# Four weight tiles with each token block at the start of a streaming encoder's first projection, in place of two

## The chip, the cores and the metric

The kernel runs on one core of a Trainium2 chip. A core has five engines, each with an instruction queue of its own that it works through in order: TensorE (PE) multiplies 128x128 tiles of weights with columns of activations into PSUM banks, VectorE (DVE) and ScalarE (ACT) work on tiles of 128 partitions, GpSimd (POOL) does small work and starts transfers, SyncE (SP) starts most transfers. The engines wait for each other through semaphores. The metric is the device time of one execution in microseconds (us), the median of several runs.

## The reference

One layer of a hybrid streaming encoder runs over 1024 prompt frames, 16 meta tokens ahead of them and 32 frames of a running stream, 1072 tokens together. All of it is in float32. The part that the change touches is the beginning:

```python
def rmsnorm(x, g):
    xf = x.astype(jnp.float32)
    r = lax.rsqrt(jnp.mean(xf * xf, axis=-1, keepdims=True) + EPS)
    return (xf * r).astype(x.dtype) * g

def project(h, w_in):
    z = h @ w_in
    a_in, q, k, v = jnp.split(z, [2 * D_CONV, 2 * D_CONV + D_ATTN, 2 * D_CONV + D_ATTN + D_KV], axis=-1)
    glu = a_in[..., :D_CONV] * jax.nn.sigmoid(a_in[..., D_CONV:])
...
def conv_module(glu_ext, dw_w, dw_b, ln_g, ln_b):
    y = depthwise_causal_conv(glu_ext, dw_w, dw_b)
    return jax.nn.silu(layernorm(y, ln_g, ln_b))
```

Each token is normalized by the root of its mean square over 1024 channels and projected to 1792 columns: 1024 for a gated unit (512 gates, 512 values), 512 for queries, 128 for keys and 128 for values. The gated unit goes through a causal convolution over 31 tokens for each channel; queries, keys and values go through windowed attention. An output projection, a gated feed-forward part and a last norm follow; the change leaves these alone.

## The kernel before

Activations are held with channels on the partitions and tokens along the columns. The 1792 columns of the first projection are 14 weight tiles of 128 columns; each has eight pieces `k` of 128 channels. Tiles 0 to 7 are gates and values of the gated unit in turn (an even tile a gate, the odd one behind it its value), 8 and 9 keys and values, 10 to 13 queries. The tokens are three blocks, `TB`: block 0 has 336 columns, block 1 has 384, block 2 has 352.

To come near float32, every operand is split into a high part (rounded to TensorE's fast format) and a low part (what the rounding left). A product is three matmuls: high by high, high by low, low by high (L252 to L254). ACT makes a high part, DVE the low part. For a weight tile of the first loads that is `split` (L246, L247); for x, multiplied by the norm's gain, it is L338 and L339. For later weight tiles, `wsplit` has ACT write the high part and the negated source (L237, L241), and a transfer started by GpSimd adds the source to it (L242).

The norm's factor isn't applied to x ahead of the projection but to its result. So the matmuls start without it, but no result can leave PSUM until it is there. For each block ACT squares the eight pieces of x (L359) and DVE adds seven of the squares into a row of sums (L362). Then `rms_first`, driven by `RM`, does three things in PE's order: three matmuls with ones sum over the partitions (L268, called the sums here), with the root taken by DVE and GpSimd behind them (L271 to L279); ACT scales the identity by the factor (L283, the diagonals); three matmuls with ones spread the factor over all partitions (L289, the spread), and ACT copies it to `rb` (L349). `RM` gives, for each block, the slots at which these happen; a slot is one `k` of one weight tile and block.

`START` is the order of the first groups: tiles 0 and 1 with block 0 side by side, then tile 0 with blocks 1 and 2, then tile 1 with blocks 1 and 2. Behind that, tiles go in `ORDER`, each with blocks 0, 1, 2, and each fetched two ahead. `NPRE` tiles stand ahead of the attention, the last two run inside of it. A finished group waits in `pend`; `flush` takes it out of PSUM once the block's factor is there (`in_evac`): a gate is multiplied by the factor (L572), goes through a sigmoid on ACT (L574) and is multiplied by the factor again (L631), then the value is multiplied by it (L577).

The convolution is 31 multiply-adds on DVE for each channel tile and stretch of tokens, the taps (L397, L400), queued in `tapq` and let out by budgets: `TGS` in the start, `TGW` behind it, with 1000.0 for all that are there. Some taps of channel tile 0 go through ACT and a GpSimd transfer (`chain_taps`, one after each group of the blocks in `CHG`).

PE's order is written out by hand in the start, and from `region` behind it on PE's and ACT's. Elsewhere a scheduler orders each engine's queue by a simulated timeline; DVE's order is always the scheduler's. SP's loads go out in the order of L330 to L332: two half weight tiles, two pieces of x, two half tiles, six more pieces of x, then blocks 1 and 2.

Of the kernel before, what the change touches and what calls it, by code (L numbers as in the profile page):

```python
# [166 lines left out]
def body(nc, tc, cp, wp, xp, dp, io):  # L167
# [150 lines left out]
    for i in range(WRM):  # L318
        nc.tensor.matmul(warm[:, 0:P], ones, ones, start=True, stop=True)

    nc.scalar.dma_start(prm, d.prm)
    for b, (t0, n) in enumerate(TB):
        if b == 0:
            pre = [[wp.tile([P, 1024], F32 if t == "raw" else F32R, tag=t, name=t) for t in ("raw", "whi", "wlo")]
                   for c in range(2)]
        for k in range(0, KD, 2):
            if b == 0 and k % 4 == 0:
                for c in range(2):
                    raw, hi, lo = (z[:, k * P:k * P + 512] for z in pre[c])
                    nc.sync.dma_start(raw, d.win[c, :, k:k + 4].rearrange("p a b -> p (a b)"))  # L330
                    split(hi, lo, raw)
            nc.sync.dma_start(X[b][:, k:k + 2, :], d.xT[:, k:k + 2, t0:t0 + n])  # L332
        if b == 0:
            pre = [z[1:] for z in pre]
        if b == 0:
            nc.scalar.dma_start(ident, d.cst[:, 0, :])
        for k in range(KD):
            hid[b, k] = nc.scalar.activation(HI[b][:, k, :], X[b][:, k, :], AF.Copy, scale=pcol("g1", k)).ins  # L338
            cast[b, k] = nc.vector.scalar_tensor_tensor(out=LO[b][:, k, :], in0=X[b][:, k, :], scalar=pcol("g1", k),  # L339
                                                        in1=HI[b][:, k, :].bitcast(F32), op0=ALU.mult,  # L340
                                                        op1=ALU.subtract).ins
    rms1 = []

    def rms_first(b, parts):
# [5 lines left out]
        ready.append(b)  # L350
        yield

    for b, (t0, n) in enumerate(TB):
        parts = [acc[:, p, t0:t0 + n] for p in (1, 0)[:NSUM]]
        for k in range(KD):
            sq = pd.tile([P, 384], F32, tag="sqs", name="sq", bufs=6)[:, :n]
            to = parts[k % NSUM] if k < NSUM else sq
            with tc.issue_after(hid[SQB[b]]):
                nc.scalar.activation(to, X[b][:, k, :], AF.Square)  # L359
            if k >= NSUM:  # L360
                with tc.issue_after(cast[SQD[b]]):
                    nc.vector.tensor_tensor(out=parts[k % NSUM], in0=parts[k % NSUM], in1=sq, op=ALU.add)  # L362
        rms1.append(rms_first(b, parts))

    close(cD)
    cA, pc_ = pool("ca", "left")
    CA = new(pc_, "ca", 4, T)
    cD, pd = pool("d2", "left")
    qpt = new(pd, "qp", 2, 2 * SEQ)
    qp = qpt.rearrange("p j (c a i) -> p j c a i", a=2, i=CHUNK)  # L370
    qs = new(pd, "qs", 4, NS)
    qm = new(pd, "qm", 4, NMETA)
    nc.gpsimd.memset(qm, 0.0)
    kT = new(pd, "kT", KW)
    vT = glu[:, 3, 0:KW]
    vsx = new(pd, "vsx", NS)
    bt = [new(pd, f"bt{i}", 4, SCW) for i in range(3)]
    bsm = new(pd, "bsm", 2, SSW)
    bme = new(pd, "bme", 17)
    mv = new(pd, "mv", 4, NMETA)  # L380
    va = new(pd, "va", NCH, P)
    vb = new(pd, "vb", NCH - 1, P)
    sm = new(pd, "sm", 36)
    vsa = new(pd, "vsa", P)
    vsb = new(pd, "vsb", P)
    ptb = [glu[:, 0, i * 512:i * 512 + 512].rearrange("p (a b) -> p a b", a=2) for i in range(2)]
    pb = [glu[:, 1, i * SCW:i * SCW + SCW] for i in range(2)] + [new(pd, f"pb{i}", SCW) for i in range(NPB - 2)]
    ksx = new(pd, "ksx", SSW)
# [170 lines left out]

# [3 lines left out]
    def in_evac(c, b, ps):  # L563
        t0, n = TB[b]
        r = rb[b]
        if c < 8:
            p = c // 2
            for lo_, hi_, o in pieces(b, CW - 1, SOFF):
                g = glu[:, p, o:o + hi_ - lo_]
                rs = r[:, lo_:hi_]  # L570
                if c % 2 == 0:
                    gate.append(nc.vector.tensor_tensor(out=g, in0=ps[:, lo_:hi_], in1=rs, op=ALU.mult))  # L572
                    if c in ORDER[:NPRE] or c == 0:
                        nc.scalar.activation(g, g, AF.Sigmoid)  # L574
                        defer.append((g, rs))
                else:
                    gate.append(nc.vector.tensor_tensor(out=g, in0=ps[:, lo_:hi_], in1=g, op=ALU.mult))  # L577
# [103 lines left out]
    region = tc.manual_schedule(engines={mybir.EngineType.PE})  # L681
    region.__enter__()
    for step in START:
        if step == START[-3]:
            spots += ["pt1", "pt0", "o"]
        for ps in zip(*(in_mm(b, pre[c]) for c, b in step)):
            pass
        pend += [(c, b, p) for (c, b), p in zip(step, ps)]
        flush()
        taps(TGS[step[0][1]], gate[-1].ins if gate else None)  # L690
    region.__exit__(None, None, None)
# [1133 lines left out]
```

## Time and profile before

| what | value |
|---|---|
| median of three runs | 1055.53 us (1055.09 to 1056.13) |
| the profiled execution | 1056.16 us |
| its span, first to last instruction | 1054.4 us |
| PE busy | 1031.6 us, 98% of the span |
| DVE busy | 864.4 us, 82% |
| ACT busy | 508.7 us, 48% |
| GpSimd busy | 161.2 us, 15% |
| mean granted clock of TensorE | 0.997 |

A row of a timeline gives start, length, engine, line, operation, result and operands by their names in the program, shape and count; in brackets stands the idle time ahead of it and what ended it. Matmuls overlap, so what one costs is the distance between two starts, not its length. A matmul on plain float32 operands shows as two rows of count.

### The profile page before, as it was taken

The numbers are of one execution on the slowest core, as the hardware profiler recorded it, in microseconds if no ns is written. First come the engines' busy times: TensorE is split into PE (matmuls) and PEld (weight loads), VectorE is DVE, ScalarE is ACT, GpSimd is POOL, SyncE is SP. The second block draws the span as 40 slices with busy tenths as digits, with TensorE's granted clock in tenths as the row PEclk, the third lists the DMA queues.
The fourth block names the chain that finished last, engine by engine and source line by source line (L and its number), as shares of the span: only waits on it lengthen the run. The fifth ranks groups of instructions, "written<-read, shape, count | busy, mean of one in ns | idle before, by whom it ended". The sixth has DMA issues, their size and how long they took to land.

```text
span 1054.4 us, 19959 instructions
## 1 busy us (share of the span) xinstructions
PE 1031.6 (98%) x7741; PEld 1005.2 (95%) x7741; DVE 864.4 (82%) x1643; ACT 508.7 (48%) x1068; POOL 161.2 (15%) x203
## 2 busy tenths in 40 slices
PE   9999999889999999999999999999999999999996
PEld 9999997658999999999999999999999999999996
DVE  7999998899978978888887888888778876985636
ACT  8653336897676744433333443343336722532333
POOL 1133120002425220001000000100110041000042
PEclk9999999999999999999999999999999999999998
DMA  7388673124963123243233233232326794732204
GB/s 267 89 172 165 148 153 71 41 47 65 168 156 107 65 79 102 71 139 97 71 114 120 63 102 116 88 102 88 116 81 209 241 188 122 245 125 81 61 4 162
DMA packets 69559, 123.88 MB, mean 117 GB/s; under 512 B 10448, under 2 KB 43464, under 8 KB 69464
## 3 DMA queue, kind: packets, MB, share of 16 engines
q1 hardware_dynamic: 56376, 96.78, 28.4%
q0 software_dynamic: 12128, 24.95, 13.9%
q8 instruction: 61, 1.00, 0.4%
q10 hardware_dynamic: 960, 0.87, 0.3%
q14 instruction: 34, 0.28, 0.1%
HBM read 78.90 MB, written 27.51 MB: 101 GB/s over the span
## 4 chain that ended last, share of the span: by engine, by line
PE 86%; DVE 6%; ACT 5%; DMA 2%; issue 1%; DVEq 0%; SPq 0%; ACTq 0%
PE mm L1281 53%; PE mm L252 10%; PE mm L254 10%; PE mm L253 10%; DVE acc L400 1%; ACT pb L763 1%; ACT glu L827 1%; PE R L289 1%; DMA raw<-wdn 1%; DVE bl L1218 1%; DMA raw<-woc 1%; ACT hi L338 1%; PE R L268 1%; DMA xs<-xT 0%; DMA prm<-prm 0%
## 5 line engine op out<-in xcount | busy, mean ns | idle before, releaser
L1281 PE MATMUL mm<-bh,sl 128*128 128x264 f32 (+1 forms) x912 | 214.0, 284 | 0.0
L1281 PEld LDWEIGHTS mm<-bh,sl 128*128 128x128 f32 x912 | 157.2, 188 | 0.0
L400 DVE SCALAR_TENSOR_TENSOR acc<-glu,prm,acc 128x324 f32<-128x324 f32 (+4 forms) x190 | 155.1, 844 | 1.1
L1281 PE MATMUL mm<-bl,sl 128*128 128x264 f32 (+1 forms) x424 | 121.0, 285 | 0.4 <-DVE bl L1218 0.4
L1281 PE MATMUL mm<-th,rawr 128*128 128x264 f32 x640 | 120.0, 284 | 0.0
L1281 PE MATMUL mm<-bh,wlo 128*128 128x264 f32 (+1 forms) x440 | 117.6, 284 | 0.0
L1281 PE MATMUL mm<-bh,whi 128*128 128x264 f32 (+1 forms) x440 | 112.6, 284 | 1.0 <-DVE x L1423 1.0
L1423 DVE TENSOR_TENSOR x<-x,mm 128x264 f32<-128x264 f32 (+7 forms) x238 | 76.1, 346 | 43.6 <-PE mm L1281 43.3
L252 PE MATMUL mm<-hi,whi 128*128 128x352 f32 (+3 forms) x312 | 103.9, 333 | 0.0
L254 PE MATMUL mm<-hi,wlo 128*128 128x352 f32 (+3 forms) x312 | 101.1, 324 | 0.0
L253 PE MATMUL mm<-lo,whi 128*128 128x352 f32 (+3 forms) x312 | 101.1, 324 | 0.0
L1281 PEld LDWEIGHTS mm<-th,rawr 128*128 128x128 f32 x640 | 100.4, 188 | 0.0
L1281 PE MATMUL mm<-th,sl 128*128 128x264 f32 x352 | 92.7, 284 | 0.0
L1281 PE MATMUL mm<-tl,rawr 128*128 128x264 f32 x320 | 90.8, 284 | 0.0
L1281 PEld LDWEIGHTS mm<-bh,wlo 128*128 128x128 f32 x440 | 80.6, 188 | 0.0
L1281 PEld LDWEIGHTS mm<-bl,sl 128*128 128x128 f32 x424 | 79.9, 188 | 0.6 <-DVE bl L1218 0.6
L1281 PEld LDWEIGHTS mm<-bh,whi 128*128 128x128 f32 x440 | 79.0, 188 | 1.2 <-ACT sl L1217 1.2
L1281 PE MATMUL mm<-bl,whi 128*128 128x264 f32 (+1 forms) x272 | 77.5, 285 | 0.0
L1217 ACT CAST sl<-x 128x512 fp32r<-128x512 f32 (+1 forms) x41 | 29.7, 727 | 73.6 <-DMA x<-wup 37.5
L1281 PEld LDWEIGHTS mm<-th,sl 128*128 128x128 f32 x352 | 63.8, 188 | 0.0
L1281 PEld LDWEIGHTS mm<-tl,rawr 128*128 128x128 f32 x320 | 60.3, 188 | 0.0
L252 PEld LDWEIGHTS mm<-hi,whi 128*128 128x128 f32 x312 | 58.7, 188 | 1.0 <-issue 0.6
(362 smaller groups left out, 2918.3 us busy)
## 6 DMA issues: line engine op xcount, KB each, us to landing
x<-wup SPq DMA_DIRECT2D x20, 512.0 KB, 4.4
x<-wup SPq DMA_DIRECT2D x40, 256.0 KB, 2.8
yq<-x SPq DMA_DIRECT2D x32, 264.0 KB, 2.8
wlo<-raw POOLq DMA_DIRECT2D x16, 512.0 KB, 4.6
ca<-ca POOLq DMA_DIRECT2D x18, 383.0 KB, 5.2
raw<-win SPq DMA_DIRECT2D x12, 512.0 KB, 4.4
raw<-wdn SPq DMA_DIRECT2D x12, 512.0 KB, 3.5
rb<-yq SPq DMA_DIRECT2D x10, 528.0 KB, 4.6
```

Of the source, the lines that this page charges most:

```text
L252: nc.tensor.matmul(ps, whi(k), xhi(k), start=first and i == 0, stop=False)
L253: nc.tensor.matmul(ps, whi(k), xlo(k), start=False, stop=False)
L254: nc.tensor.matmul(ps, wlo(k), xhi(k), start=False, stop=last and i == n - 1)
L268: nc.tensor.matmul(ss[:, i:i + 1], z[:, at:at + P], ones[:, 0:1], start=j == 0, stop=j == len(parts) - 1)
L289: nc.tensor.matmul(R[:, at:at + P], left[i], diag[i], start=True, stop=True)
L338: hid[b, k] = nc.scalar.activation(HI[b][:, k, :], X[b][:, k, :], AF.Copy, scale=pcol("g1", k)).ins
L400: nc.vector.scalar_tensor_tensor(out=a, in0=e[:, a0 + k:a1 + k], scalar=pcol("cw", p * CW + k), in1=a, op0=ALU.mult, op1=ALU.add)
L763: nc.scalar.activation(qs_[i], qs_[i], AF.Exp, bias=m[0][:, i:i + 1], scale=-1.0, accum_out=m[1][:, i:i + 1])
L827: nc.scalar.copy(ptb[kv], pts[kv])
L1217: nc.scalar.copy(hi, raw)
L1281: nc.tensor.matmul(ps, w[:, j, :], x[:, j, :], start=first and j + i == 0, stop=j == 3 and i == 2, skip_group_check=True)
L1423: summed[0] = nc.vector.tensor_tensor(out=z, in0=z, in1=ps[:, lo_:hi_], op=ALU.add).ins
```

## The change

Tiles 2 and 3 join tiles 0 and 1 in the start, and its order is now by block: four tiles with block 0, then four with block 1, then four with block 2. `ORDER` loses 2 and 3 and `NPRE` goes from 10 to 8, so the tiles ahead of the attention are the same. Tile 4 comes next, then 5, 8, 9, 10 and so on; before, 8 and 9 stood ahead of 4.

All first loads, splits and squares are written out, and ACT's order is by hand from the beginning. The parameters come in two transfers: the eight columns of the first gain on ACT's queue, the rest on SP's, where the identity's load goes too. Tiles 2 and 3 are split by ACT and DVE with `split`, whole. Block 1's second half of x, block 1's squares, block 2's x and block 2's squares are given to ACT at slots 27, 34, 41 and 58. There are 12 warm-up matmuls in place of 18. The budgets of taps, the slots of the norms and of the bias setup are new tables; chained taps go after every group, no longer after two of three.

```diff
-TGS = [3.0, 3.0, 1000.0, 1000.0]
+TGS = [0.0, 0.0, 0.0, 0.0, 2.0, 2.0, 2.0, 3.0, 3.0, 3.0, 3.0]
...
-BS = ((0, 2), (1, 0), (2, 1), (2, 2))
+BS = ((1, 0), (1, 1))
 PF = 7
-START = (((0, 0), (1, 0)), ((0, 1),), ((0, 2),), ((1, 1),), ((1, 2),))
-WRM = 18
+NB0 = 4
+START = (((0, 0), (1, 0)), *(((c, b),) for b in range(3) for c in range(2 if b == 0 else 0, NB0)))
+WRM = 12
...
-ORDER = [2, 3, 8, 9, 4, 5, 10, 11, 12, 13, 6, 7]
+ORDER = [4, 5, 8, 9, 10, 11, 12, 13, 6, 7]
...
-CHG = (1, 2)
+CHG = (0, 1, 2)
...
-NPRE = 10
+NPRE = 8
...
-RM = ((27, 31, 41), (45, 48, 53), (56, 59, 63))
-VR = 16
+RM = ((24, 26, 33), (48, 50, 57), (66, 68, 75))
+VR = 13
...
+    first_load(0, 0, 4)
+    x_load(0, 0)
+    first_load(1, 0, 4)
+    x_load(0, 2)
+    first_load(0, 4, 4)
+    first_load(1, 4, 4)
+    x_load(0, 4)
+    x_load(0, 6)
+    first_load(2, 0, 8)
+    x_load(1, 0)
+    x_load(1, 2)
+    first_load(3, 0, 8)
+    x_load(1, 4)
+    x_load(1, 6)
+    nc.sync.dma_start(ident, d.cst[:, 0, :])
+    nc.sync.dma_start(prm[:, KD:], d.prm[:, KD:])
+    for k in range(0, KD, 2):
+        x_load(2, k)
...
+    squares(0)
+    first_split(3, 0, 8)
+    x_split(1, 0, 4)
+    later_acts = {27: lambda: x_split(1, 4, 8), 34: lambda: squares(1), 41: lambda: x_split(2, 0, 8),
+                  58: lambda: squares(2)}
...
+            later_acts.pop(slot[0], lambda: None)()
             slot[0] += 1
```

The diff moves rows on every engine. Lines of the changed kernel are one less than before up to the splits some 14 to 16 more in the projection behind them, and 41 more in the attention: its sums are L267, its spread L288, its squares L393 on ACT and L395 on DVE, its gates L587 and L646, its values L592, its taps L411 and L414.

DVE, the third norm. In the kernel before, the additions of block 2's squares (`sq` of 352 columns into `acc`) stand like this, ahead of the first tap:

```order
L362 TENSOR_TENSOR acc<-acc,sq 128x384 x3
L362 TENSOR_TENSOR acc<-acc,sq 128x352 x6
L572 TENSOR_TENSOR glu<-mm,rb 128x336
L362 TENSOR_TENSOR acc<-acc,sq 128x352
L271 TENSOR_SCALAR stat<-R 128x3
L515 TENSOR_SCALAR bt_291<-acc 128x4
```

In the changed kernel they stand behind four taps that follow the second norm, and among the evacuation of block 1's first two tiles (`pt_349` and `mm` are their gates, `pt_409` the first value):

```order
L587 TENSOR_TENSOR glu<-pt_349,rb 128x384
L587 TENSOR_TENSOR glu<-mm,rb 128x384
L414 SCALAR_TENSOR_TENSOR acc<-glu,prm,acc 128x324
L395 TENSOR_TENSOR acc<-acc,sq 128x352
L826 MEMSET pt_1710 128x512
L395 TENSOR_TENSOR acc<-acc,sq 128x352 x2
L646 TENSOR_TENSOR glu<-glu,rb 128x384
L395 TENSOR_TENSOR acc<-acc,sq 128x352
L646 TENSOR_TENSOR glu<-glu,rb 128x384
L592 TENSOR_TENSOR glu<-pt_409,glu 128x384
L395 TENSOR_TENSOR acc<-acc,sq 128x352
L592 TENSOR_TENSOR glu<-mm,glu 128x384
```

A tap, a memset, the sixth addition, a tap and the seventh addition follow these rows. So the seven additions have moved from one run, ahead of the taps, to places among ten other operations.

PE, the place that waits for them. Before, block 2's sums come three matmuls into tile 2 with block 1, when all three blocks have been multiplied with tiles 0 and 1, and block 0 with tile 2:

```order
L252 MATMUL mm<-hi_85,whi 128x384
L253 MATMUL mm<-lo_86,whi 128x384
L254 MATMUL mm<-hi_85,wlo 128x384
L268 MATMUL R<-ones,acc 128x1 x3
L252 MATMUL mm<-hi_85,whi 128x384
L253 MATMUL mm<-lo_86,whi 128x384
```

Now they come nine matmuls into the first tile with block 2 (`hi_83` and `lo_84` are block 2's high and low part):

```order
L251 MATMUL mm<-hi_83,whi 128x352
L252 MATMUL mm<-lo_84,whi 128x352
L253 MATMUL mm<-hi_83,wlo 128x352
L267 MATMUL R<-ones,acc 128x1 x3
L251 MATMUL mm<-hi_83,whi 128x352
L252 MATMUL mm<-lo_84,whi 128x352
```

The sums have moved from behind two tiles with all blocks to just behind the eight groups of blocks 0 and 1.

ACT, between the norms. Before, all of x is split and the squares of all blocks stand in the first forty rows or so, with the diagonals put among them. In the changed kernel, from tile 3's cast to the second norm's diagonals:

```order
L245 CAST whi_135<-raw_134 128x1024
L342 ACTIVATE hi_85<-xs_107,prm 128x384 x4
L282 ACTIVATE diag_96<-ident,stat 128x128
L282 ACTIVATE diag_97<-ident,stat 128x128
L282 ACTIVATE diag_98<-ident,stat 128x128
L342 ACTIVATE hi_85<-xs_107,prm 128x384 x4
L379 COPY rb<-R 128x336
L393 ACTIVATE acc<-xs_107 128x384
L393 ACTIVATE sq<-xs_107 128x384 x7
L589 ACT_TABLE_LOAD
L589 ACTIVATE glu<-glu 128x336 x2
L342 ACTIVATE hi_83<-xs_108,prm 128x352 x8
```

The squares of block 1 have moved behind the first norm's copy, and block 2's pieces behind the first sigmoids. The second norm's diagonals, its copy and the squares of block 2 follow.

More of the change, by code (lines that the diff above doesn't have):

```diff
@@ L52 @@
 NPB = 8
-TGS = [3.0, 3.0, 1000.0, 1000.0]
-TGW = [3.0, 5.0, 6.5, 3.5, 1000.0, 1000.0, 5.0, 1000.0, 1000.0, 1000.0, 3.5, 3.5, 1000.0, 1000.0, 1000.0, 1000.0, 1000.0, 1000.0, 3.0, 3.0, 1000.0, 1000.0, 1000.0, 1000.0, 1000.0, 1000.0, 7.0, 3.5, 3.5, 3.5]
+TGS = [0.0, 0.0, 0.0, 0.0, 2.0, 2.0, 2.0, 3.0, 3.0, 3.0, 3.0]
+TGW = [3.5, 3.5, 3.5, 3.5, 1000.0, 1000.0, 5.0, 1000.0, 1000.0, 1000.0, 3.5, 3.5, 3.0, 3.0, 1000.0, 1000.0, 1000.0, 1000.0, 1000.0, 1000.0, 7.0, 3.5, 3.5, 3.5]
 TA = [2.01, 2.74, 5.63, 6.64, 4.22, 3.28, 2.42, 2.68, 2.08, 1.57, 2.08, 2.08, 3.18, 1.41, 2.1, 0.85, 4.71, 3.21, 5.98, 2.57]
@@ L103 @@
 NSUM = 1
-SQB = ((1, 7), (2, 7), (2, 7))
-SQD = ((0, 7), (2, 7), (2, 7))
-RM = ((27, 31, 41), (45, 48, 53), (56, 59, 63))
-VR = 16
+RM = ((24, 26, 33), (48, 50, 57), (66, 68, 75))
+VR = 13
 BW = SEG + 2 * NMETA
@@ L319, in body @@
         nc.tensor.matmul(warm[:, 0:P], ones, ones, start=True, stop=True)
[L321 to L341, printed above, removed]
@@ new lines, in body, with first_load @@
+    region = tc.manual_schedule(engines=MANUAL)
+    region.__enter__()
+    nc.scalar.dma_start(prm[:, 0:KD], d.prm[:, 0:KD])
+    first = [[wp.tile([P, 1024], F32 if t == "raw" else F32R, tag=t, name=t) for t in ("raw", "whi", "wlo")]
+             for c in range(2)]
+    first += [[new(pd, f"{t}{c}", 1024, dt=F32 if t == "raw" else F32R) for t in ("raw", "whi", "wlo")]
+              for c in range(2, NB0)]
+    pre = [z[1:] for z in first]
+    def first_load(c, k, n):
+        nc.sync.dma_start(first[c][0][:, k * P:(k + n) * P], d.win[c, :, k:k + n].rearrange("p a b -> p (a b)"))
@@ new lines, in first_split, with x_load, x_split @@
+    def first_split(c, k, n):
+        raw, hi, lo = (z[:, k * P:(k + n) * P] for z in first[c])
+        split(hi, lo, raw)
+    def x_load(b, k):
+        t0, n = TB[b]
+        nc.sync.dma_start(X[b][:, k:k + 2, :], d.xT[:, k:k + 2, t0:t0 + n])
+    def x_split(b, k0, k1):
+        for k in range(k0, k1):
+            nc.scalar.activation(HI[b][:, k, :], X[b][:, k, :], AF.Copy, scale=pcol("g1", k))
+            nc.vector.scalar_tensor_tensor(out=LO[b][:, k, :], in0=X[b][:, k, :], scalar=pcol("g1", k),
+                                           in1=HI[b][:, k, :].bitcast(F32), op0=ALU.mult, op1=ALU.subtract)
@@ new lines, in body @@
+    first_load(0, 0, 4)
[16 more added lines that the diff above has]
+        x_load(2, k)
+    first_split(0, 0, 4)
+    x_split(0, 0, 2)
+    first_split(1, 0, 4)
@@ L342, in body @@
+    x_split(0, 2, 4)
+    first_split(0, 4, 4)
+    first_split(1, 4, 4)
+    x_split(0, 4, 8)
+    first_split(2, 0, 8)
     rms1 = []
@@ L351, in rms_first, with parts_of, squares @@
         yield
-    for b, (t0, n) in enumerate(TB):
-        parts = [acc[:, p, t0:t0 + n] for p in (1, 0)[:NSUM]]
+    def parts_of(b):
+        t0, n = TB[b]
+        return [acc[:, p, t0:t0 + n] for p in (1, 0)[:NSUM]]
+    def squares(b):
+        parts = parts_of(b)
+        n = TB[b][1]
         for k in range(KD):
@@ L357, in body @@
             to = parts[k % NSUM] if k < NSUM else sq
-            with tc.issue_after(hid[SQB[b]]):
-                nc.scalar.activation(to, X[b][:, k, :], AF.Square)
+            nc.scalar.activation(to, X[b][:, k, :], AF.Square)
             if k >= NSUM:
[L361 to L388, printed above, removed]
+                nc.vector.tensor_tensor(out=parts[k % NSUM], in0=parts[k % NSUM], in1=sq, op=ALU.add)
+    rms1 += [rms_first(b, parts_of(b)) for b in range(3)]
+    squares(0)
[3 more added lines that the diff above has]
+                  58: lambda: squares(2)}
     tapq, spare = [], [0.0, 0]
@@ L572, in in_evac @@
                     gate.append(nc.vector.tensor_tensor(out=g, in0=ps[:, lo_:hi_], in1=rs, op=ALU.mult))
-                    if c in ORDER[:NPRE] or c == 0:
+                    if c != 6:
                         nc.scalar.activation(g, g, AF.Sigmoid)
@@ L679, in v_rows @@
                 yield
[L681 to L691, printed above, removed]
     order = ORDER
@@ L707, in body @@
     fetch()
-    region = tc.manual_schedule(engines=MANUAL)
-    region.__enter__()
-    nxt = take()
+    for i, step in enumerate(START):
+        if i == 2:
+            spots += ["pt1", "pt0", "o"]
+        gens = [in_mm(b, pre[c]) for c, b in step]
+        ps = [None] * len(step)
+        for k in range(0, KD, 2):
+            for j, g in enumerate(gens):
+                for _ in range(2):
+                    ps[j] = next(g)
+        pend += [(c, b, p) for (c, b), p in zip(step, ps)]
+        flush()
+        taps(TGS[i], gate[-1].ins if gate else None)
+        if step[0] == (1, 2):
+            nxt = take()
+        if step[0][1] == 2 and step[0][0] > 1:
+            next(bias_steps)
+    close(cD)
+    cA, pc_ = pool("ca", "left")
+    CA = new(pc_, "ca", 4, T)
+    cD, pd = pool("d2", "left")
+    qpt = new(pd, "qp", 2, 2 * SEQ)
+    qp = qpt.rearrange("p j (c a i) -> p j c a i", a=2, i=CHUNK)
+    qs = new(pd, "qs", 4, NS)
+    qm = new(pd, "qm", 4, NMETA)
+    nc.gpsimd.memset(qm, 0.0)
+    kT = new(pd, "kT", KW)
+    vT = glu[:, 3, 0:KW]
+    vsx = new(pd, "vsx", NS)
+    bt = [new(pd, f"bt{i}", 4, SCW) for i in range(3)]
+    bsm = new(pd, "bsm", 2, SSW)
+    bme = new(pd, "bme", 17)
+    mv = new(pd, "mv", 4, NMETA)
+    va = new(pd, "va", NCH, P)
+    vb = new(pd, "vb", NCH - 1, P)
+    sm = new(pd, "sm", 36)
+    vsa = new(pd, "vsa", P)
+    vsb = new(pd, "vsb", P)
+    ptb = [glu[:, 0, i * 512:i * 512 + 512].rearrange("p (a b) -> p a b", a=2) for i in range(2)]
+    pb = [glu[:, 1, i * SCW:i * SCW + SCW] for i in range(2)] + [new(pd, f"pb{i}", SCW) for i in range(NPB - 2)]
+    ksx = new(pd, "ksx", SSW)
     vr = v_rows()
```

## The prediction

> **What bounds the kernel now.** I read the page first, then the timeline of each engine up to the attention part, since every edit lies ahead of it.
>
> ```profile
> span 1054.4 us, 19959 instructions
> ...
> PE   9999999889999999999999999999999999999996
> ...
> PEclk9999999999999999999999999999999999999998
> ...
> PE 86%; DVE 6%; ACT 5%; DMA 2%; issue 1%; DVEq 0%; SPq 0%; ACTq 0%
> ...
> wlo<-raw POOLq DMA_DIRECT2D x16, 512.0 KB, 4.6
> ```
>
> TensorE (PE) is busy in every slice, and the chain that ended last is 86% PE. So PE is the bound, and a change in the first projection is worth what it does to the moments at which PE has nothing to do there. The profiled execution took 1056.16 us, 1.76 more than its span.
>
> ```profile
> 1.06 6.92 PE L319 MATMUL warm<-ones 128*128 128x128 f32 x36 [1.06 <-DVE ones L194]
> 7.74 0.40 PE L252 MATMUL mm<-hi,whi 128*128 128x336 f32 x1
> ...
> 15.26 0.34 PE L252 MATMUL mm<-hi,whi 128*128 128x384 f32 x1
> ...
> 19.42 0.32 PE L252 MATMUL o<-hi,whi 128*128 128x352 f32 x1
> ...
> 22.45 0.82 PE L268 MATMUL R<-ones,acc 128*128 128x1 f32 x6
> 23.13 0.41 PE L252 MATMUL o<-hi,whi 128*128 128x352 f32 x1
> ...
> 43.94 1.07 PE L289 MATMUL R<-diag,ones 128*128 128x128 f32 x6
> 44.77 0.41 PE L252 MATMUL mm<-hi,whi 128*128 128x352 f32 x1
> 45.02 0.32 PE L253 MATMUL mm<-lo,whi 128*128 128x352 f32 x1
> ...
> 48.54 0.32 PE L254 MATMUL mm<-hi,wlo 128*128 128x352 f32 x1
> 48.79 0.81 PE L461 MATMUL line<-acc 32*8 32x384 f32 x2
> ```
>
> This is PE's timeline. From start to start a projection matmul takes (15.26-7.74)/48 = 0.157 us for block 0, (19.42-15.26)/24 = 0.173 for block 1, (48.54-45.02)/22 = 0.160 for block 2. A norm costs PE 0.68 for the three sums (L268) and 0.83 for the three spreads (L289). After 48.79 PE runs on without a wait worth naming until the attention part:
>
> ```profile
> 163.88 0.18 DVE L756 CUSTOM_DVE_ANT_0 glu<-S,bme 128x17 f32<-128x17 f32 x1 [0.23 <-PE S L855]
> ```
>
> VectorE (DVE) waits for PE there, so DVE isn't behind when the attention begins.
>
> **The break-even.** The work is the same before and after; only its order differs. I take one place, the sums of block 2's norm (the third R row of PE; L267 in the changed kernel). PE reaches it after 96 matmuls of block 0, 96 of block 1, 9 of block 2 and both pieces of two norms. Before, at 48.79, PE had done 72 of each and both pieces of three. The difference is -24 x 0.157 - 24 x 0.173 + 63 x 0.160 + 1.51 = 3.67 us. So before stood at the same amount of work at 48.79 - 3.67 = **45.1 us**. Whatever the changed kernel is later than 45.1 with these sums, it is later at the end, since the rest of PE's order is the same.
>
> **When the sums come: the rows.** They wait for the last addition of squares on DVE. These are its rows, and then ScalarE's (ACT):
>
> ```profile
> 9.15 1.29 DVE L247 TENSOR_TENSOR wlo<-raw,whi 128x512 fp32r<-128x512 f32 x2
> 10.40 6.24 DVE L339 SCALAR_TENSOR_TENSOR lo<-xs,prm,hi 128x336 fp32r<-128x336 f32 x12
> 16.60 2.96 DVE L362 TENSOR_TENSOR acc<-acc,sq 128x336 f32<-128x336 f32 x5
> 19.48 1.07 DVE L339 SCALAR_TENSOR_TENSOR lo<-xs,prm,hi 128x352 fp32r<-128x352 f32 x2
> 20.48 0.50 DVE L362 TENSOR_TENSOR acc<-acc,sq 128x336 f32<-128x336 f32 x1
> 20.89 1.07 DVE L339 SCALAR_TENSOR_TENSOR lo<-xs,prm,hi 128x352 fp32r<-128x352 f32 x2
> ...
> 24.29 0.15 DVE L271 TENSOR_SCALAR stat<-R 128x3 f32<-128x3 f32 x1
> 24.36 1.21 DVE L362 TENSOR_TENSOR acc<-acc,sq 128x384 f32<-128x384 f32 x2
> 25.69 0.16 DVE L276 SCALAR_TENSOR_TENSOR stat<-stat 128x3 f32<-128x3 f32 x1
> ...
> 40.24 0.55 DVE L631 TENSOR_TENSOR glu<-glu,rb 128x384 f32<-128x384 f32 x1
> 40.71 0.55 DVE L400 SCALAR_TENSOR_TENSOR acc<-glu,prm,acc 128x324 f32<-128x324 f32 x1
> 41.18 0.55 DVE L577 TENSOR_TENSOR glu<-pt,glu 128x384 f32<-128x384 f32 x1
> ...
> 42.37 0.48 DVE L785 MEMSET pt<- 128x512 f32 x1
> 42.76 0.15 DVE L277 TENSOR_TENSOR stat<-stat 128x3 f32<-128x3 f32 x1
> ...
> 45.54 0.59 DVE L572 TENSOR_TENSOR glu<-o,rb 128x320 f32<-128x320 f32 x2
> ```
>
> ```profile
> 4.50 0.62 ACT L246 CAST whi<-raw 128x512 fp32r<-128x512 f32 x1 [1.55 <-DMA raw<-win]
> ...
> 6.47 2.14 ACT L338 ACTIVATE hi<-xs,prm 128x336 fp32r<-128x336 f32 x4 [0.44 <-DMA xs<-xT]
> ...
> 16.10 2.34 ACT L359 ACTIVATE sq<-xs 128x336 f32<-128x336 f32 x6
> ...
> 26.26 1.04 ACT L237 CAST whi<-raw 128x1024 fp32r<-128x1024 f32 x1
> ...
> 29.32 0.97 ACT L283 ACTIVATE diag<-ident,stat 128x128 f32<-128x128 f32 x3
> ...
> 32.18 1.28 ACT L574 ACT_TABLE_LOAD   x1
> ```
>
> On DVE, start to start: half a weight tile's low part 0.62, a whole one 1.24 as two halves; a token piece's low part 0.52; a gate, an evacuation or a short tap 0.47; a memset 0.39. An addition of squares takes 0.58 behind another (16.60 to 19.48, five) and 0.41 where other work stands between (20.48 to 20.89). A norm's step through GpSimd costs 1.40 (24.29 to 25.69). ACT needs 0.39 for a square of block 0 (I take 0.41 for the wider block 1), 0.51 for a piece of x (four in 2.14, the last to its end) and 1.28 for its table.
>
> **The chain, step by step** (estimates from these rows).
>
> First norm. ACT's first cast waits for weights until 4.50; with the parameters cut to 8 columns and the identity moved back, 0.2 MB less is ahead of them, so about 4.05. The first piece of x landed at 6.47 behind 1.1 MB; now it comes behind 0.66, and at 0.37 MB a us (the next row) that is 1.2 less, 5.2. ACT's 0.56 on it gives the first matmul at about 5.8 in place of 7.74; the 12 warm-up matmuls, in place of 18, are over by then (two thirds of 6.92 from 1.06). Tile 2's weights are moved as the last of 2.95 MB:
>
> ```profile
> GB/s 0 29 180 305 316 367 381 382 370 382 393 401 396 400 396 396 405 381 355 406 341 25 9 9 0 0 8 0 0 0 197 197 131 0 152 375 153 9 156 201
> ```
>
> One number is one us; they reach 2.95 MB at 10.6, and about 0.6 later it is there. ACT casts it (1.04), and DVE starts its split at 12.4. From there to the norm's last addition DVE has this split (1.24), five additions (2.9), tile 3's split (1.24), an addition (0.41), three pieces of block 1 (1.56) and the seventh addition (0.50): the sums can start at 20.2. PE could be there at 5.8 + 75 x 0.157 = 17.6. **A wait of up to 2.6.** Bounds: if DVE never waits for loads, its four half splits and eight pieces (6.6) run from 4.7 and the sums come at 19.2; as late as before (22.45) is the other end. I take the middle one, since the loads' row is of this same stretch.
>
> Second norm. PE's 0.68, DVE's and GpSimd's 1.4 and two more small steps reach ACT's diagonals at 22.9. ACT now has the order fixed: diagonals 0.9, four pieces of block 1 at 0.51, the copy of R, eight squares at 0.41, the table 1.28, a sigmoid. DVE's next gate stands behind that until 31.3, and two additions, two gates, an evacuation and a piece of block 2 follow (2.9): sums of block 1 at 34.2. PE gets there with 0.68, 21 x 0.157, 6 x 0.173, 0.83 and 45 x 0.173 from 20.2, at 33.8. **A wait of 0.4.**
>
> Its spread. DVE takes six pieces of block 2, an evacuation and a tap (3.9), then 1.40, then three taps with the small steps between (1.1): the diagonals at 40.4, the spread at 40.9. PE could be there at 34.2 + 0.68 + 27 x 0.173 = 39.6. **A wait of 1.3.**
>
> Third norm. From the spread to the first evacuation took 1.60 before (43.94 to 45.54), so 42.5. Then DVE's order, the first piece of it shown with the change, holds ahead of the last addition's end: two evacuations and a tap 1.41, two memsets 0.78, two gates 0.94, two evacuations 0.94, two taps 0.94, seven additions 3.2 (five at 0.41, one at 0.58 and the last to its end). Sum 8.2, with the hand-over to PE 8.4: **50.9**. PE, with 0.83 + 18 x 0.173 + 9 x 0.160 = 5.4 from 40.9, stands there at 46.3. **A wait of 4.6**, and the firmest of the four: both sides start from the same spread and neither depends on how the loads went.
>
> 50.9 - 45.1 = **+5.8 us**. The other way round: 8.9 of waits come, the start gives 1.9 back, and 1.2 by difference is before's own small gaps in these 45 us.
>
> **What I cost at nothing.** Tile 4's low part still goes through GpSimd: the third spread comes near 56, the gates some 2.5 behind, two casts of 1.04 after them, so it is issued near 60.6 and lands 4.6 later at 65.2, while PE wants it at 50.9 + 0.68 + 0.83 + 87 x 0.160 and the line product, at 67. Without this cover of 2 us PE would wait for what is missing of it, once. The bias loads and their use move together. The tap budgets move taps among DVE's free moments behind 52; DVE waited for PE at 163.88 with PE earlier, and PE now comes later. The identity and the remaining parameters move to SP behind block 1's loads; at some 0.39 MB/us they land near 17, first wanted at 22.9. No later order on PE changes.
>
> [...] The longest wait of PE for another engine before is this:
>
> ```profile
> PE o L836 <- ACT ca L844: 5.2, 9, 1.7
> ```
>
> 1.7 us, and the granted clock stays full beside it; a wait of 4.7 isn't in this trace.
> [...]
>
> **Rivals.**
> - *The clock drops in the long wait.* Before has no wait that long, so nothing speaks against it. For every us in which matmuls run at half rate PE loses half; for 4 us, a good half of the warm-up row's 6.92, that is 2 more: 1063.3. Chance 0.17. [...]
> - *Part comes back in the attention.* PE waits there on ACT and DVE, and these may run ahead by what PE lost. For: the attention is bound by them. Against: DVE was already waiting for PE at 163.88, and the order from there on is almost the same. If half returns: +3, 1058.4; all of it: no change. Chance 0.13.
> - *The faster start carries through.* The place is DVE's queue between the second spread and the third norm's last addition. If it is through by 45.1, the kernel is no slower; if PE never waits there, the sums come at 5.8 + 15.1 + 16.6 + 1.4 + 3.0 = 41.9, which is -3.2: 1052.3. DVE would have to do 8.2 us of work and the 1.6 ahead of it in the 5.4 that PE needs; for it speaks only that more of DVE's first pieces come earlier. Chance 0.08.
>
> **How the numbers follow.** The forecast has 0.62. The runs' median is 1055.53, so 1055.53 + 5.8 = **1061.3 us** (the profiled execution: 1062.0). From below the range takes in half of the attention rival and a first norm at its early bound with a shorter third wait: 1058. From above it takes in the clock rival and a late first norm: 1064.5. A measurement of this kernel tells 0.2%, about 2.1 us, from no change. Faster 0.08 is the last rival; same 0.09 is the larger part of the attention rival; the rest, 0.83, is slower.
>
> **What would show it.** Among PE's waits, R (L267) on DVE's additions (L395) with the longest near 4.6 and some 7.6 in all, and R (L288) on a diagonal near 1.3. First matmul near 5.8. The third R at 50.9, and the row that is at 163.88 near 169.7. DVE without idle from 31 to 51. Wrong would be: no wait at the third R, or the attention starting late and the span not.

## The result and the profile after

The changed kernel takes **1067.55 us** (median of 4 runs, 1067.06 to 1070.53), the kernel before 1055.31 beside it (4 runs, 1054.32 to 1056.13): 1.0123 times as long, 95% interval 1.0111 to 1.0136. The forecast had the sign and the place, and half of the size: +5.8 foretold, +12.2 measured. The profiled execution took 1067.56 us.

The page of the changed kernel, span, busy tenths and granted clock in 40 slices, and the chain that ended last:

```profile
span 1065.8 us, 19931 instructions
...
PE   8799999898999999999999999999999999999996
...
PEclk9989999999999999999999999999999999999998
...
PE 83%; DVE 6%; ACT 5%; DMA 2%; issue 2%; SPq 0%; POOL 0%; DVEq 0%; ACTq 0%
```

The slices are 26.6 us each, and the chain row has PE at 83% for 86% before. What is new against before stands in the first three: PE has 8, 7 and 9 tenths there, and the clock row has an 8 in the third slice where before had 9 throughout.

The waits of PE in the changed kernel (in total, times, longest):

```profile
PE R L267 <- DVE acc L395: 7.3, 3, 4.9
...
PE R L288 <- ACT diag L282: 2.5, 2, 1.4
```

The first row is the forecast's: 7.3 in three waits, the longest 4.9, against 7.6 and 4.6 foretold. So the waits came as expected, and they cannot be the missing 6 us. PE's timeline has it:

```profile
5.73 0.40 PE L251 MATMUL mm<-hi,whi 128*128 128x336 f32 x1
...
21.01 0.83 PE L267 MATMUL R<-ones,acc 128*128 128x1 f32 x6 [1.66 <-DVE acc L395]
21.70 0.40 PE L251 MATMUL o<-hi,whi 128*128 128x336 f32 x1
...
23.04 0.48 PE L251 MATMUL o<-hi,whi 128*128 128x336 f32 x1
...
27.59 0.83 PE L288 MATMUL R<-diag,ones 128*128 128x128 f32 x6
...
36.98 0.80 PE L267 MATMUL R<-ones,acc 128*128 128x1 f32 x6 [0.75 <-DVE acc L395]
...
43.68 1.07 PE L288 MATMUL R<-diag,ones 128*128 128x128 f32 x6 [1.10 <-ACT diag L282]
...
54.20 1.41 PE L267 MATMUL R<-ones,acc 128*128 128x1 f32 x6 [4.87 <-DVE acc L395]
55.48 0.64 PE L251 MATMUL mm<-hi,whi 128*128 128x352 f32 x1
...
175.38 0.29 PE L896 MATMUL S<-kT,qm 64*64 64x17 f32 x4
```

The attention's first product in the kernel before:

```profile
163.54 0.29 PE L855 MATMUL S<-kT,qm 64*64 64x17 f32 x4
```

Two things are to be seen. From start to start a matmul of block 0 takes 0.28 us around 23 (21 of them, and 6 of block 1, fill the 5.89 between 21.70 and 27.59; at the rates of before that is 4.33); behind the third wait the sums take 1.28 (54.20 to 55.48) instead of 0.68. And the attention's first product stands at 175.38, against 163.54: 11.84 later. The spans differ by 11.4. So all of the loss lies ahead of the attention, and next to nothing comes back there.

The granted clock says why. This view sums each engine's busy time in a stretch (its length, then PE, weight loads, DVE, ACT, GpSimd); the last three columns are granted clock, DMA share and GB/s, and I cut the stretches at the moments at which the clock changes, to 0.04 us:

```profile
18.84:22.25 3.41, 1.75 (x14) 1.48 (x13) 2.81 (x7) 0.40 (x1) 0.13 (x1) 1.00 1.06 361
22.25:25.67 3.42, 3.42 (x15) 3.42 (x14) 1.00 (x4) 2.03 (x6) 0.76 (x1) 0.50 0.53 191
...
49.56:52.97 3.41, 0.00 (x0) 0.00 (x0) 3.31 (x8) 0.00 (x0) 0.00 (x0) 1.00 0.00 0
52.97:56.38 3.41, 2.18 (x9) 2.21 (x10) 3.30 (x9) 0.00 (x0) 0.48 (x1) 0.50 0.00 0
56.38:59.80 3.42, 3.42 (x14) 3.42 (x13) 2.88 (x8) 0.99 (x3) 0.62 (x1) 0.50 0.00 0
59.80:63.21 3.41, 3.41 (x25) 3.41 (x24) 0.00 (x0) 0.45 (x1) 0.00 (x0) 1.00 0.00 0
```

In three stretches of 3.41 us the granted clock is 0.50: once behind the wait of only 1.66, twice behind that of 4.87. Before has 1.00 throughout from 20 to 163.5 us.

### The profile page after: what moved, and what is told of

Same layout as the page of the kernel before. It is cut to its first block, busy times and chain, and to the rows that moved or that the text cites. A ratio compares the mean times of both kernels' runs of the same rounds, so it can differ in the third digit from the quotient of the medians.

```text
span 1065.8 us, 19931 instructions
## 1 busy us (share of the span) xinstructions
PE 1037.1 (97%) x7729; PEld 1009.4 (95%) x7729; DVE 865.8 (81%) x1645; ACT 507.7 (48%) x1066; POOL 159.9 (15%) x201
## 4 chain that ended last, share of the span: by engine, by line
PE 83%; DVE 6%; ACT 5%; DMA 2%; issue 2%; SPq 0%; POOL 0%; DVEq 0%; ACTq 0%
PE mm L1322 51%; PE mm L251 10%; PE mm L252 10%; PE mm L253 10%; DVE acc L414 2%; ACT pb L804 1%; ACT glu L868 1%; DMA raw<-win 1%; PE R L288 1%; DMA raw<-wdn 1%; PE R L267 1%; DMA raw<-woc 1%; ACT sq L393 1%; DVE acc L395 0%; DVE bl L1259 0%
## 5 line engine op out<-in xcount | busy, mean ns | idle before, releaser
L414 DVE SCALAR_TENSOR_TENSOR acc<-glu,prm,acc 128x1090 f32<-128x1090 f32 (+4 forms) x190 | 154.0, 843 | 0.8
L252 PEld LDWEIGHTS mm<-lo,whi 128*128 128x128 f32 x312 | 59.8, 192 | 0.9 <-DVE lo L343 0.7
```

Of the source, the lines that this page charges most:

```text
L252: nc.tensor.matmul(ps, whi(k), xlo(k), start=False, stop=False)
L414: nc.vector.scalar_tensor_tensor(out=a, in0=e[:, a0 + k:a1 + k], scalar=pcol("cw", p * CW + k), in1=a, op0=ALU.mult, op1=ALU.add)
```

## The experiments

Two theories stood at the start. **Clock theory**: some 4 us of the excess are matmuls at half clock behind PE's waits. **Order theory**: what DVE and ScalarE have queued sets when each norm comes, so that slow matmuls are hidden and only waits cost. The added lines shift line numbers by 1 to 4 in some kernels (sums L268, spread L289, additions L399). Ratios are to the kernel before, with 95% intervals.

### Matmuls that fill the third wait

```diff
+FILLW = {2: 20}
...
-        rms = rms_steps(parts, b * 9, D, pa.tile([P, 512], F32, tag="s2", name="R", bufs=2))
+        R = pa.tile([P, 512], F32, tag="s2", name="R", bufs=2)
+        for _ in range(FILLW.get(b, 0)):
+            nc.tensor.matmul(R[:, 0:P], ones, ones, start=True, stop=True)
+        rms = rms_steps(parts, b * 9, D, R)
```

> 20 matmuls of ones on ones go ahead of block 2's sums, so PE works through most of its 4.87 us there; nothing else is changed. Clock theory (the granted clock falls because PE stands still, and the matmuls behind the wait pay for it): the clock stays full from 53 to 60 us, the sums still start near 54.2, the three sums take 0.68 in place of 1.28 and the 27 matmuls behind them 4.3 us in place of 6.4, so the kernel is 2.7 us faster than the changed one, near 1064.9. Order theory (only the waits cost; what runs behind them is waited for elsewhere anyway): no gain, 1067.5, or later if the added matmuls outlast the wait.

Measured: **1062.78** (1.0072, 1.0047 to 1.0097), 4.8 less than the changed kernel. PE's timeline:

```profile
20.48 0.83 PE L268 MATMUL R<-ones,acc 128*128 128x1 f32 x6 [1.70 <-DVE acc L399]
...
48.64 4.62 PE L378 MATMUL R<-ones 128*128 128x128 f32 x40
53.58 0.83 PE L268 MATMUL R<-ones,acc 128*128 128x1 f32 x6 [0.31 <-DVE acc L399]
...
172.19 0.29 PE L900 MATMUL S<-kT,qm 64*64 64x17 f32 x4
```

From the third sums to the attention it is 118.61 us (172.19 - 53.58); in the changed kernel 121.18 (175.38 - 54.20); before, counted from the break-even place, 118.44 (163.54 - 45.1). Work that is thrown away, put into a wait, saves **2.57 us**, where 2.7 was expected, and the granted clock is 1.00 from 26 us up to the attention: the clock theory holds for the third wait. The rest of the gain in the median isn't resolved with times that range from 1060.94 to 1065.94.

### The first wait too: 6 matmuls, then 3

```diff
-FILLW = {2: 20}
+FILLW = {0: 6, 2: 20}
```

> As the run with 20 added matmuls, and 6 more ahead of block 0's sums, in PE's first wait of 1.66 us. Clock theory: the clock is full all through 20 to 60 us, the first spread starts at 26.0 in place of 27.6, the second and third norm move up by that 1.6, and the time is 4.3 us below the changed kernel's, near 1063.2. Order theory: DVE's queue sets the third sums at 54.2 wherever the first spread stands, 1067.5 or a little later.

Measured: **1063.72** (1.0082, 1.0063 to 1.0102). That is near the 1063.2 of the clock theory by luck only, since what was expected on the way didn't come. The first spread did come earlier, at 25.52, but block 1's sums stayed, and the drop moved there (0.50 from 38.27 to 41.68):

```profile
25.52 0.83 PE L289 MATMUL R<-diag,ones 128*128 128x128 f32 x6
36.30 0.80 PE L268 MATMUL R<-ones,acc 128*128 128x1 f32 x6 [2.15 <-DVE acc L399]
```

DVE's order is not written out in this part; the compiler puts it together by its own idea of times, and with six matmuls more it had put block 1's last addition three rows later. So two things had changed. With three added matmuls the order up to the third sums is the changed kernel's:

```diff
-FILLW = {0: 6, 2: 20}
+FILLW = {0: 3, 2: 20}
```

> 20 added matmuls ahead of block 2's sums as before, and 3 (not 6) ahead of block 0's: with 6 the compiler also put three other rows of DVE ahead of block 1's last addition, so that run did not show what the first wait's slow matmuls cost; with 3 DVE's order up to block 2's sums is the changed kernel's. If the slow matmuls behind the first wait are on the path: the clock stays full there, the first spread comes near 25.5 in place of 27.06, block 1's sums near 34.8 in place of 36.44, block 2's near 52, and the time is 1.5 us below the run with 20 alone, near 1061.3. If 0.75 us of added work is too little to hold the clock, or DVE hides the loss: as that run, 1062.8.

Measured: **1062.48** (1.0071, 1.0052 to 1.0091).

```profile
20.52 0.83 PE L268 MATMUL R<-ones,acc 128*128 128x1 f32 x6 [1.03 <-DVE acc L399]
25.58 0.83 PE L289 MATMUL R<-diag,ones 128*128 128x128 f32 x6
...
34.96 0.80 PE L268 MATMUL R<-ones,acc 128*128 128x1 f32 x6 [0.74 <-DVE acc L399]
...
52.09 0.83 PE L268 MATMUL R<-ones,acc 128*128 128x1 f32 x6 [0.31 <-DVE acc L399]
...
170.70 0.29 PE L900 MATMUL S<-kT,qm 64*64 64x17 f32 x4
```

From the first to the third sums: 31.57, against 33.10 with the third wait alone filled and 33.19 in the changed kernel. The slow matmuls behind the first wait cost **1.5 us**, all of which reaches the third sums (52.09) and the attention (170.70): with three matmuls, a row of 0.83 us, the clock is 1.00 from 17.02 to 27.26, where it was 0.50 from 22.04 to 25.45 with the third wait alone filled. The profiled executions differ by 1.95 (1062.17 against 1064.12), the medians by only 0.3; the four times of each kernel range over 1061.47 to 1064.36 and 1060.94 to 1065.94, which can't resolve 1.5. The scatter behind the attention's start is large in itself: in this profile two stretches of the attention had a clock of 0.50 (from 194 and 232 us), in the other one (from 196).

### PE takes the norms up later

```diff
-RM = ((24, 26, 33), (48, 50, 57), (66, 68, 75))
+RM = ((28, 30, 38), (50, 52, 61), (76, 78, 85))
```

> The slots at which PE takes up the norms are later by the length of the waits: block 0's sums and spread by 4, 4 and 5 slots (1.9 us), block 1's by 2, 2 and 4, block 2's by 10 (4.8 us). PE has projection matmuls to do where it stood still. If the waits (and the clock that falls behind them) are the whole loss: no wait over 0.5 us ahead of the attention, full clock, third sums near 49, and the start's 1.9 us is a gain: 1052 to 1056. If DVE's amount of work ahead of block 2's gates is what counts, the waits come back at another place (a tile of PSUM that no gate has freed, or a later norm) and the time is 1060 to 1067.

Measured: **1057.41** (9 runs; 1.0022, 1.0012 to 1.0032), 10 us less than the changed kernel.

```profile
40.45 1.07 PE L288 MATMUL R<-diag,ones 128*128 128x128 f32 x6 [0.49 <-ACT diag L282]
...
49.21 0.80 PE L267 MATMUL R<-ones,acc 128*128 128x1 f32 x6 [0.39 <-DVE acc L395]
...
57.20 0.40 PE L251 MATMUL mm<-hi,whi 128*128 128x352 f32 x1 [0.36 <-DVE glu L587]
...
163.34 0.29 PE L896 MATMUL S<-kT,qm 64*64 64x17 f32 x4
```

The clock is 1.00 up to 188 us, no wait is over 0.5, and the attention begins at 163.34, 0.2 ahead of before. So the change loses its time because PE is led to the norms too early, not because four tiles per block are slower. But it also gains nothing: the first matmul is at 6.20, 1.54 ahead of before, and 1.24 of that goes in the three waits shown. Its span is 0.4 longer than before's all the same (1054.8 against 1054.4); one stretch of the attention, from 188 us, has a clock of 0.52 in this profile, and none is below 1.00 in that of before. The expected 1052 to 1056 was too low.

### What holds block 2's sums

```diff
-TGS = [0.0, 0.0, 0.0, 0.0, 2.0, 2.0, 2.0, 3.0, 3.0, 3.0, 3.0]
+TGS = [0.0, 0.0, 0.0, 0.0, 0.0, 0.0, 0.0, 3.0, 3.0, 3.0, 3.0]
```

> The tap budgets of block 1's four steps are 0 in place of 2.0, so nine short taps leave DVE's queue ahead of block 2's last addition, about seven of them (3.3 us) behind the second spread's statistics. If DVE's order sets the third sums: they start 2 to 3.3 us earlier, at 51 to 52, PE's wait there is 1.6 to 2.9, and the kernel is 2 to 4 us faster than the changed one (the larger end if the clock then stays full), 1063.5 to 1065.5. If ScalarE's squares or the gates set the sums: no more than 1 us.

Measured: **1064.90** (1.0090, 1.0070 to 1.0111).

```diff
-                  58: lambda: squares(2)}
+                  51: lambda: squares(2)}
```

> The changed kernel with block 2's squares issued on ScalarE at slot 51 in place of 58; nothing else. DVE then has block 2's last addition ahead of a gate, a memset and two taps (1.8 us). If DVE's order ahead of that addition sets PE's third wait: the sums start near 52 in place of 54.2, the wait is about 2.7, and the time 2 to 4 us below the changed kernel's. If the copy of R, now 3.3 us later on ScalarE behind the squares, holds the gates and with them everything: no gain, 1067.

Measured: **1064.89** (1.0095, 1.0080 to 1.0110). The third sums of the first kernel, and then of the second:

```profile
51.49 0.90 PE L267 MATMUL R<-ones,acc 128*128 128x1 f32 x6 [4.13 <-DVE acc L395]
```

```profile
51.64 0.80 PE L267 MATMUL R<-ones,acc 128*128 128x1 f32 x6 [3.09 <-DVE acc L395]
```

From the first sums (20.11 and 20.22) that is 31.4 in both, against 33.19: 1.8 less. In the second kernel block 1's spread stands where it stood (22.66 behind the first sums, for 22.67), and what left DVE's queue ahead of the last addition, a value, a memset and two taps, is the 1.8. In the first, nine taps are gone, but the sums don't gain what these cost. Its spread comes 1.1 earlier and without a wait, and behind it only 0.7 is won, since DVE then stands idle for 2.11 us until ScalarE has copied the factor to `rb`. PE is early by as much, so its wait is 4.13 and not the 1.6 to 2.9 expected. The step of the prediction that has DVE's queue set the third wait holds, with that copy as the next limit. Both kernels then have one stretch at 0.50 behind this wait (from 52.09 and from 52.91) in place of two.

### The faster start alone

In the kernel before, first only with the parameters cut, the identity moved and 12 warm-up matmuls:

```diff
-WRM = 18
+WRM = 12
...
-    nc.scalar.dma_start(prm, d.prm)
+    nc.scalar.dma_start(prm[:, 0:KD], d.prm[:, 0:KD])
...
-        if b == 0:
-            nc.scalar.dma_start(ident, d.cst[:, 0, :])
+        if b == 1:
+            nc.sync.dma_start(ident, d.cst[:, 0, :])
+            nc.sync.dma_start(prm[:, KD:], d.prm[:, KD:])
```

> The kernel before with the new start alone: 8 parameter columns first, the identity and the other columns behind block 1's loads, 12 warm-up matmuls. Two tiles per block stay. If the start's gain carries through by itself: first matmul near 5.8, 1.9 us less, 1053.6. If DVE's squares and pieces of x hold what follows: PE waits near 17 to 22 us for what it won, and the time is 1055.5.

Measured: **1057.60** (10 runs; 1.0021, 1.0011 to 1.0031), slower by 0.2%. x still came behind both weight halves; PE had done its 12 matmuls and waited 2.30 until 7.75, and the clock fell to 0.51:

```profile
4.08:7.49 3.41, 1.37 (x12) 1.18 (x11) 1.29 (x2) 1.56 (x3) 0.00 (x0) 1.00 0.92 287
7.49:10.90 3.41, 3.15 (x10) 2.83 (x11) 3.17 (x6) 3.01 (x7) 0.00 (x0) 0.51 1.04 376
```

Then with the changed kernel's order of the first loads as well:

```diff
...
+            for c, k in ((0, 0), ("x", 0), (1, 0), ("x", 2), (0, 4), (1, 4), ("x", 4), ("x", 6)):
...
```

> The kernel before with the changed kernel's order of the first loads: the first tile's half, a piece of x, the second tile's half, a piece of x, and so on; parameters cut and the identity moved as in the run with the parameters alone, where x stayed behind both halves and came at 7.75 all the same. If the start's gain carries through: first matmul near 5.9, 1.8 us less, 1053.5, and no half clock ahead of the attention. If DVE's pieces of x and squares hold PE: waits of 0.3 to 1 between 19 and 23 us, and 1055.2.

Measured: **1056.59** (12 runs; 1.0013, 1.0004 to 1.0021). PE's timeline:

```profile
6.00 0.42 PE L252 MATMUL mm<-hi,whi 128*128 128x336 f32 x1 [0.47 <-ACT hi L341]
...
19.84 0.43 PE L253 MATMUL o<-lo,whi 128*128 128x352 f32 x1 [0.71 <-DVE lo L342]
...
22.18 0.82 PE L268 MATMUL R<-ones,acc 128*128 128x1 f32 x6
```

PE starts 1.74 earlier, waits for DVE's pieces of x, and is at the first sums 0.27 earlier (22.18 against 22.45). The start's gain is no gain of the kernel: DVE comes behind PE by nearly as much. The time is 0.13% longer than before's even so; in this profile one stretch of the attention, from 188.6 us, had a clock of 0.50, but no run here shows that this is the reason.

### Versions that should have beaten both

Later slots and zero budgets together:

```diff
-TGS = [0.0, 0.0, 0.0, 0.0, 2.0, 2.0, 2.0, 3.0, 3.0, 3.0, 3.0]
+TGS = [0.0, 0.0, 0.0, 0.0, 0.0, 0.0, 0.0, 3.0, 3.0, 3.0, 3.0]
...
-RM = ((24, 26, 33), (48, 50, 57), (66, 68, 75))
+RM = ((28, 30, 38), (50, 52, 61), (76, 78, 85))
```

> The later slots for the norms (28, 30, 38; 50, 52, 61; 76, 78, 85) together with no taps in block 1's steps. In the run with the later slots PE still lost 0.49 and 0.39 us at block 1's spread and block 2's sums and 0.36 at a tile that a gate freed late, with taps ahead on DVE each time. If those taps are the cause, the three go and the time is 1 us below that run, 1056.4; if the taps are then late at the attention, no gain, 1057.4 or more.

Measured: **1064.11** (1.0081, 1.0065 to 1.0098), 6.7 more than with the later slots alone. The attention does begin early, at 161.26, and then PE waits (the waits of PE in two stretches, 120 to 180 us and 240 to 400):

```profile
PE pt L861 <- DVE glu L812: 1.5, 1, 1.5
PE pt L903 <- ACT glu L814: 1.4, 1, 1.4
...
PE mm L251 <- ACT rbg L1223: 3.6, 1, 3.6
```

The first of these is 1.0 in the kernel before. What stands ahead of the second and the third, on DVE and then on PE and ScalarE:

```profile
162.68 2.61 DVE L414 SCALAR_TENSOR_TENSOR acc<-glu,prm,acc 128x1090 f32<-128x1090 f32 x2
165.20 0.16 DVE L809 RECIPROCAL sm<-sm 128x1 f32<-128x1 f32 x1
...
348.76 0.83 PE L288 MATMUL R<-diag,ones 128*128 128x128 f32 x6
...
352.67 0.46 ACT L1223 COPY rbg<-R 128x384 f32<-128x384 f32 x1
```

The 1.4 is taps that come late: ScalarE has the sum of the attention's weights at 163.7, and DVE takes its reciprocal only behind two taps. The 3.6 isn't. It stands at a later norm, and ScalarE copies that norm's factor 3.9 us behind the spread in the kernel before too (347.51 and 351.41). There PE's next matmuls don't wait for the copy (they start at 348.09); here they do. Why they do here is open.

Then block 2's squares earlier as well, and its slots with them:

```diff
-RM = ((28, 30, 38), (50, 52, 61), (76, 78, 85))
+RM = ((28, 30, 38), (50, 52, 62), (72, 74, 81))
...
-                  58: lambda: squares(2)}
+                  51: lambda: squares(2)}
```

> As the last one, and block 2's squares issued on ScalarE at slot 51 in place of 58, with block 2's slots at 72, 74, 81. DVE then has block 2's additions ahead of block 1's gates. If the whole loss was that DVE came late with block 2's last addition: no wait of PE over 0.3 us from 8 to 90, the start's gain of 1.5 to 1.9 carries through to the attention, 1053.5 to 1055. If block 1's gates, now behind those additions, come too late for the tiles that PE needs: a wait there of 0.5 us or more and 1056 to 1058.

Measured: **1062.52** (6 runs; 1.0067, 1.0054 to 1.0081): no wait over 0.2 ahead of the attention, which begins at 161.21, and the same 1.4 and 3.6 behind. Of the lead of 2.3 nothing is left at 216 us (the same matmul of the attention starts at 215.57, and at 215.56 in the kernel before), and at the spread ahead of the 3.6 the two are still level (347.40 and 347.51). So what this kernel loses begins with the 3.6, the larger part of the 5.4 between the spans (1059.8 and 1054.4). Last, these slots and squares with the change's own budgets:

```diff
-TGS = [0.0, 0.0, 0.0, 0.0, 0.0, 0.0, 0.0, 3.0, 3.0, 3.0, 3.0]
+TGS = [0.0, 0.0, 0.0, 0.0, 2.0, 2.0, 2.0, 3.0, 3.0, 3.0, 3.0]
```

> The changed kernel with block 2's squares at slot 51, the norms' slots at 28, 30, 38; 50, 52, 62; 72, 74, 81, and the tap budgets left as the change has them (2.0 in block 1's steps; with 0 there the attention began at 161.2 but waited 1.4, 1.5 and 3.6 us for taps that were then late). If the taps were all that was lost there: attention near 161.5, those waits gone, 1053.5 to 1055. If a lead of 2 us at the attention always meets DVE behind: waits there of 1 to 3 us, 1056 to 1058.

Measured: **1057.83** (12 runs; 1.0022, 1.0014 to 1.0031). The 3.6 is gone, but the attention begins only at 163.38, mostly since PE now waits 1.19 at block 1's spread. So the versions with zero budgets and the later slots reach the attention 2.3 earlier and more than give it back. The last expectation puts all of that down to late taps; the rows show it for the 1.4 and against it for the 3.6, which the run with zero budgets and the old slots doesn't have either. No version here beats the kernel before.

## Why the prediction was right in sign and wrong in size

**The break-even place** (right). Full-clock runs need 118.61 from the third sums to the attention, the prediction's place implied 118.44.

**The waits** (right but for the first). Third 4.87 for 4.6, block 1's spread 1.10 for 1.3, block 1's sums 0.75 for 0.4, first sums 1.66 for "up to 2.6". The first is shorter as PE came later: it lost time in small waits at the start and was there at 19.35, not 17.6. The two kernels with less ahead of the last addition confirm that DVE's queue sets the third.

**"The granted clock stays full beside it"** (wrong; this is the step that failed). From one row, a wait of 1.7 us in the attention, the prediction took it that a wait of that length costs no more than itself, and left the clock out of the sum. It stood only as a rival of 0.17, priced at 2 behind the long wait alone. That the clock falls behind the long wait was the author's assumption: before's profile has a fall only at 1047.68, to 0.50 at the kernel's end. The 4 us at half rate in that price are in no run; the runs showed 0.50 for two stretches of 3.41 us behind the third wait and for one behind the first. The fills measure 2.57 there and 1.5 behind the first wait, 4.1 together.

**The first norm's chain** (right, but for a late load). Sums at 21.01, not 20.2: +0.8. ScalarE's timeline has a wait for the second tile's weights that the chain didn't hold:

```profile
7.07 0.62 ACT L245 CAST whi<-raw 128x512 fp32r<-128x512 f32 x1 [0.95 <-DMA raw<-win]
```

The other nine profiles with this start have this cast at 5.86 to 6.30 without a wait, and the five of them in which PE waits at the first sums have these at 20.1 to 20.5. So most of the 0.8 belongs to this one execution.

**The chains of the second and third norm** (mis-sized). At full clock 31.57 from the first to the third sums, where the steps gave 30.7 (50.9 - 20.2): +0.9.

Together at the attention: 5.8 foretold, 4.1 clock, 0.8 for the late load, 0.9 for the other two chains, 0.2 behind the third sums: 11.8, and 11.84 was measured.

**The rivals.** "Part comes back in the attention": no; +11.84 at its start, +11.4 at the end. "The faster start carries through": no, and not for the reason given alone. Without PE's waits (later slots) the kernel reaches the attention as before, not 3.2 earlier, as DVE and ScalarE hold PE in small waits; and where PE does get there 2.3 earlier, the lead is gone by 216 us, in part to taps that DVE hasn't done yet.

**The range** ended at 1064.5, which is the clock rival's 1063.3 and 1.2 for a late first norm: it held one wait with a lower clock behind it, and there were two (0.50 from 22.28 and from 53.00).

## What to carry to other kernels

Price a wait on TensorE with what runs behind it: here a wait of 1.66 us cost 1.5 more and one of 4.87 cost 2.6 more, and idle matmuls in the wait brought that back. A consumer that is placed too early in a hand-written order costs more than one placed a little late: moving PE's norm slots by 2 to 10 slots was worth 10 us, while what the faster start won was lost again further on. And where a compiler orders an engine, compare its order before reading an experiment: three rows of DVE hid the answer of one run here.

## What the runs showed of the hardware

In the changed kernel's profile the clock changes only at whole multiples of 3.41 us, and the length of a wait doesn't decide alone. The moments are 22.28, 25.70, 53.00, 59.83, 199.78 and 203.19, and 1056.52 where the clock falls at the end; the first six are 1, 8, 2, 41 and 1 times 3.4133 apart within 0.01 us, where 3.4133 is (1056.52 - 22.28)/303. What goes with a fall is how little PE was busy in the stretch that ends there. Some such stretches with the one behind them: of the run with 6 and 20 matmuls, of that with zero budgets, and of the kernel before (its boundaries counted back by 253 times 3.4133 from 1047.68, where its clock falls at the end):

```profile
34.86:38.27 3.41, 1.97 (x13) 2.00 (x14) 3.41 (x8) 1.29 (x3) 0.00 (x0) 1.00 0.02 5
38.27:41.68 3.41, 3.41 (x12) 3.41 (x12) 3.22 (x11) 0.07 (x1) 1.10 (x1) 0.50 0.00 0
```

```profile
45.26:48.68 3.42, 2.10 (x13) 1.81 (x11) 3.11 (x8) 1.96 (x5) 0.00 (x0) 1.00 0.00 0
48.68:52.09 3.41, 0.60 (x6) 0.63 (x6) 3.27 (x8) 0.00 (x0) 0.00 (x0) 1.00 0.00 0
52.09:55.50 3.41, 3.41 (x13) 3.41 (x14) 2.88 (x9) 0.25 (x1) 1.15 (x1) 0.50 0.00 0
```

```profile
184.11:187.52 3.41, 1.75 (x14) 1.22 (x12) 1.15 (x5) 3.40 (x13) 0.00 (x0) 1.00 0.00 0
187.52:190.93 3.41, 2.98 (x22) 2.23 (x23) 2.84 (x10) 3.41 (x9) 0.85 (x1) 1.00 0.00 0
```

The first number behind the stretch's length is PE's busy time. In all thirteen profiles of this case, from 7 to 256 us, each stretch with 1.74 or less was followed by 0.50 to 0.52; from full clock none with 2.0 or more was; between them it went either way: 1.75 was followed by 0.50 in the changed kernel (18.84 to 22.25) and by 1.00 in before, 1.97 by 0.50 in the run with 6 and 20 matmuls, 1.95 by 1.00 in that with the later slots and zero budgets (169.19 to 172.60). So the attention's wait of 1.7, the row on which the prediction rested, was a narrow escape: in before it left 1.75 us of work in its stretch and the clock stayed at 1.00; in the changed kernel the same wait left 1.69 (196.33 to 199.74) and the next 3.41 us had 0.51, as behind the same wait in ten more of the thirteen profiles (1.70, then 0.50 to 0.52). Where the boundaries lie differs from run to run: counted back to the start of the span they come at 1.80 us in the changed kernel, 3.20 in before and 0.72 in the run with 6 and 20 matmuls. That this makes up the scatter of such kernels (1060.94 to 1065.94 in the run with 20 matmuls) is a guess of the author's that no run shows.
